# Down sums on another DMA queue, gated rows stored by quarters, and weights prepared a step earlier, in a decoder layer on one core

## The chip, the core and the metric

The kernel runs on one core of a Trainium2 chip. TensorE (PE) multiplies, VectorE (DVE), ScalarE (ACT) and GpSimd (POOL) work beside it, and SyncE (SP) issues most transfers between DRAM and the core's own memory; POOL issues the rest. The metric is the device time of one execution, in microseconds (us). The time before is 1876.97 us, the median of three runs (1875.70 to 1879.47).

## What is computed

One layer of a decoder, for a prompt of 1024 tokens and, with the same weights, for a group of 8 samples of one token each; together 1032 columns. Three branches (a gated linear recurrence, windowed attention, attention into a memory) are projected, gated and merged, and a gated feed-forward part follows. The change lies in that last part:

```python
D_MODEL, D_FF = 1024, 2816        # D_FF = 22 blocks of 128

def decoder_layer(x, ...):
    ...
    h = layer_norm(ALPHA * x + merged @ w_out, ln1_g, ln1_b)
    gt, up = jnp.split(h @ w_gate_up, 2, axis=-1)
    h = layer_norm(ALPHA * h + (jax.nn.silu(gt) * up) @ w_down, ln2_g, ln2_b)
    return h, conv_new, h_new, wk_new, wv_new
```

## The kernel before

**Layout and products.** Activations stand transposed, 128 features by 1032 columns. Each fp32 operand is split into a high and a low part: ACT casts the high part (L84), DVE subtracts it to get the low one (L85). A product is then three matmuls (high by high, high by low, low by high), each of 128 x 128 weights against 258 columns, a quarter of the 1032.

**Fast products.** A product of two by two blocks is made with seven block products in place of eight, of sums of weight blocks and sums of operand blocks; `fast_quarter` prepares the weights of one of the seven, i = 0 to 6, and `fast_step` multiplies and adds them up. In the gate and up projection two neighbouring units u = ("g", f) and v = ("g", f + 1), f even, share further products by the same scheme: `second_quarter`/`second_step` (steps "p0", "p1", "p4", "p6") and `fifth_quarter`/`fifth_step` ("v0", "v1", "v4", "v6"). Such a pair runs as

    (u,0) (prev v4) (u,1) (prev v6) (u,2) p0 (u,4) p1 (u,6) (v,0) p4 (v,1) p6 (v,2) v0 (v,4) v1 (v,6)

and takes about 39 us. "Pair 10" below is the pair with f = 10 and 11.

**The stage.** `gate_up_down` (L1600) works through pairs f = 2 to 21, then through the down products of blocks 0 to 15, in two parts of eight blocks. It fills about 1240 to 1790 us of the span. Its loop issues, at each step, the preparation of the weights `ahead` = 3 steps later (`quarter`), then the step's matmuls, then what falls due. Every engine works in the order in which it was issued; that order is fixed when the kernel is built. The prepared weights sit in rotating places: tag "qh" five, tag "ql" four, and one more "ql" in another pool (`half_pair`, L108).

**Gated rows.** When a unit's gate and up rows are complete, `FinishGate.done` (L2057) applies silu on ACT, multiplies on DVE (L2058) and stores the row, 128 x 1032, to DRAM (`scr["f"]`, L2059, on SP).

**Down sums.** The fast down product needs its operands, blocks of four rows by 258 columns, and sums of them. `down_block` (L1544) loads a block from four stored rows, in pieces of 258 columns (1032 bytes). `down_sums(part)` (L1551) is a generator: for p = 0 and 1 it loads b11, b12, b22, subtracts (L1563, L1565), stores, loads b21, adds (L1570), subtracts (L1573) and stores; the stores go to `scr["t"]` (L1558). Part 0 starts at f = 8 and part 1 at f = 16; a piece is issued after steps (u,2), (u,4) and (v,0). The first subtractions thus fall in pairs 8, 10, 16 and 18, after (v,0). All its loads and stores are on SP's queue. They use slots of `zt`, nine buffers of 128 x 1032 that gated rows use too, so a load into a slot waits until the store that last read it has landed. Later `down_operand` (L1579) loads blocks and sums for the product.

**What stands around it.** In `fast_step` at (v,0) DVE runs L389, which takes the result of earlier products out of PE's accumulator bank "pd" (tile pdfg). PE's product p4 (L1525 to L1527) begins a new sum in that bank and waits for L389. Blocks of a further scratch `t5` are loaded by `fifth_load` (L1417) for the products at L1465. `weight_means` (L1768) loads, in eight pieces of 128 x 768 into zt slots, the weights of the last six blocks and reduces them on DVE (L1777). Raw weights are loaded at L265.

Of the kernel before, what the change touches and what calls it, by code (L numbers as in the profile page):

```python
# [10 lines left out]
F32 = mybir.dt.float32  # L11
F32R = mybir.dt.float32r
# [7 lines left out]
P = 128  # L20
D = 1024
# [39 lines left out]
class Builder:  # L61
# [338 lines left out]
    def project(self, ctx, pool):  # L400

        nc, io, tc = self.nc, self.io, self.tc
        self.qdc = self.cst.tile([P, KT * NB], F32, name="qdc")
        self.qds = self.cst.tile([P, KT * NB], F32, name="qds")
        self.kd = self.cst.tile([P, 2 * NB], F32, name="kd")
        self.vd = self.cst.tile([NB, 256], F32, name="vd")
        self.lru_setup()
# [234 lines left out]
    def mem_scores(self, h, half, q, mk, between):  # L642

        nc = self.nc
        out = []
        for pr in range(2):
            s = self.bank("s", f"cs{h}_{half}_{pr}")
            for u in range(2):
                qt = pr * 2 + u
                self.mm3(s[:, u * 256:(u + 1) * 256], [  # L650
                    ((q[j][0][:, qt * P:(qt + 1) * P], q[j][1][:, qt * P:(qt + 1) * P]), mk[j]) for j in range(2)
                ])
            st = self.sm.tile([P, 8], F32, tag="cst", name=f"cst{h}_{half}_{pr}", bufs=4)
            p = self.ph.tile([P, 4 * 129], F32, tag="p", name=f"cp{h}_{half}_{pr}", bufs=4)[:, :512]
            nc.vector.tensor_reduce(st[:, 0:2], s.rearrange("p (a b) -> p a b", b=256), axis=AX.X,
                                    op=ALU.max, negate=True)
            for u in range(2):
                nc.scalar.activation(p[:, u * 256:(u + 1) * 256], s[:, u * 256:(u + 1) * 256], AF.Exp,
                                     bias=st[:, u:u + 1], scale=1.0, accum_out=st[:, 2 + u:3 + u])
            nc.vector.reciprocal(st[:, 4:6], st[:, 2:4])  # L660
            for u in range(2):
                nc.vector.tensor_scalar_mul(p[:, u * 256:(u + 1) * 256], p[:, u * 256:(u + 1) * 256],
                                            st[:, 4 + u:5 + u])
            out.append(p)
            if pr == 0:
                between()
        return out
# [108 lines left out]
    def win_scores(self, kv, ops, b, between=lambda: None):  # L776
# [6 lines left out]
        snk = self.nsnk[:, 4 * kv:4 * kv + 4]  # L783
        st = self.sm.tile([P, 12], F32, tag="bst", name=f"bst{kv}_{b}", bufs=4)
        p = self.ph.tile([P, 4 * 129], F32, tag="p", name=f"bp{kv}_{b}", bufs=4).rearrange("p (g n) -> p g n", g=4)
# [126 lines left out]
    def lru_consts(self):  # L912

        nc = self.nc
        lam = self.vec[:, V_LAM:V_LAM + KT]
        w = self.cst.tile([P, 8 * KT], F32, name="lruc")
# [3 lines left out]
        self.nsnk = self.cst.tile([P, 16], F32, name="nsnk")  # L920
        nc.vector.tensor_scalar_mul(self.nsnk, self.vec[:, V_SNK:V_SNK + 16], -1.0)
        self.hbg = self.cst.tile([P, 24], F32, name="hbg")
        nc.vector.tensor_scalar_mul(self.hbg, self.vec[:, V_BG:V_BG + 24], 0.5)
# [16 lines left out]
        nc.vector.tensor_scalar_mul(self.sp2, t, 2.0)  # L940
        self.sp4n = self.cst.tile([P, KT], F32, name="sp4n")
        nc.vector.tensor_scalar_mul(self.sp4n, t, -4.0)

    def lru_setup(self):
        self.scv = self.cst.tile([P, KT, 3, NB], F32, name="scv")
        self.scvo = self.cst.tile([P, KT, 3, NB], F32, name="scvo")
        self.sh = self.cst.tile([P, KT, NB], F32, name="sh")
        self.sho = self.cst.tile([P, KT, NB], F32, name="sho")
        self.pconv = self.cst.tile([P, KT, 3], F32, name="pconv")
        self.pho = self.cst.tile([P, KT], F32, name="pho")  # L950

# [83 lines left out]
    def dec_rows(self, qd, m0, dr, name):  # L1035

        nc = self.nc
        rows = self.sm.tile([NB, 256], F32, tag="drow", name=f"drow_{name}{m0}", bufs=1)
        ps = self.bank("o", f"drt_{name}{m0}")
# [5 lines left out]
    def dec_mem(self, h):  # L1045
# [45 lines left out]
        pr = ph.tile([NB, 256], F32, tag="dp", name=f"dcp{h}", bufs=1)  # L1091
        st = self.sm.tile([P, 8], F32, tag="cst", name=f"dcst{h}", bufs=4)
        nc.vector.tensor_reduce(st[:NB, 0:1], ps[:NB, :256], axis=AX.X, op=ALU.max, negate=True)
# [31 lines left out]
    def dec_win(self):  # L1125
# [7 lines left out]
        for name, row in (("o_swk", krow), ("o_swv", self.vd)):  # L1133
            nc.sync.dma_start(io[name][:, P - 1, :], row)
        work = self.sm.tile([P, 256], F32, tag="drow", name="dwork", bufs=1)
        qb, sc = work[:, :P], work[:, P:]
# [29 lines left out]
        pr = qb  # L1166
        st = self.sm.tile([P, 8], F32, tag="cst", name="dsst", bufs=4)
        snk = self.vec[:, V_SNKD:V_SNKD + 1]
# [8 lines left out]
        nc.vector.tensor_scalar_mul(sc, self.ident, pr[:, 0:1])  # L1177
        own = self.sm.tile([P, 8], F32, tag="cst", name="down", bufs=4)
        nc.vector.tensor_reduce(own, self.ident.rearrange("p (b r) -> p b r", b=NB), axis=AX.X, op=ALU.add)
# [148 lines left out]
    def plain_gate_up(self, f, h, steps):  # L1328
# [5 lines left out]
        for q in range(4):  # L1334
# [15 lines left out]
        nc.sync.dma_start(self.scr["f"][:, f, :], out)  # L1350
        self.zfree(out)
# [191 lines left out]

    def down_block(self, part, kh, th, p):  # L1544

        t = self.zt(f"f{part}{kh}{th}{p}")
        f0, t0 = 8 * part + 4 * kh, HT * th + QN * p
        self.nc.sync.dma_start(t.rearrange("p (k n) -> p k n", k=4), self.scr["f"][:, f0:f0 + 4, t0:t0 + QN])
        return t

    def down_sums(self, part):  # L1551


        tt = self.nc.vector.tensor_tensor
        for p in range(2):

            def keep(i, t):
                self.nc.sync.dma_start(self.scr["t"][:, part, p, (1, 2, 4, 6).index(i), :], t)  # L1558

            b11, b12 = (self.down_block(part, 0, th, p) for th in range(2))  # L1560
            b22 = self.down_block(part, 1, 1, p)
            yield
# [4 lines left out]
            self.zfree(b12)  # L1567
            b21 = self.down_block(part, 1, 0, p)
            yield
# [30 lines left out]
    def gate_up_down(self, ts):  # L1600
# [28 lines left out]
        todo = deque()  # L1629
        ahead = 3  # L1630

# [103 lines left out]
    def last_rows(self, home, j0):  # L1735

        flat = lambda t: t.rearrange("p k n -> p (k n)")
        for p, pair in enumerate(self.slot_pairs(home, f"g{home}")):
            hi, lo = map(flat, pair)
            self.nc.sync.dma_start(lo.bitcast(F32), self.scr["f"][:, LAST[0] + j0 + p, :])  # L1740
            self.g.append((hi, lo))
# [221 lines left out]
    def build(self):  # L1963
# [21 lines left out]
        with ExitStack() as right:  # L1985
            slots = right.enter_context(ExitStack())
            self.slots = [slots.enter_context(pool("slots0", "right"))]
            with pool("acc") as acc, pool("gp") as self.gp:
# [23 lines left out]
                with pool("slots1") as slots1:  # L2012
# [32 lines left out]
class FinishGate:  # L2045
# [9 lines left out]
    def done(self, za, zb):  # L2055
        b, nc = self.b, self.b.nc
        nc.scalar.activation(za, za, AF.Silu)  # L2057
        nc.vector.tensor_mul(za, za, zb)  # L2058
        nc.sync.dma_start(b.scr["f"][:, self.f, :], za)  # L2059
        b.zfree(za, zb)  # L2060
# [164 lines left out]
```

## Time and profile before

| | |
|---|---|
| median of three runs | 1876.97 us |
| the profiled execution, its own time | 1878.54 us |
| its span in the trace | 1876.8 us |
| granted TensorE clock, mean | 0.998 |
| DVE in the stage, 1240 to 1780 us | 416.2 of 540 us busy |
| blocks for down sums and products, loaded on SP (L1548) | 28 of 516 KB |
| POOL in the stage | 21 instructions, 18.0 us |

A busy time is the sum of an engine's instructions in the profiled execution. In a timeline a row has the start in us, the length in us, engine, line, operation, tile written and tiles read, their sizes, and in brackets the idle time of the engine just before and what ended it. "DMA to landing" is the time from the issue of a transfer until its last byte has landed, as minimum, median and maximum of a group. Tile names are the program's without numbers: z is a zt slot, pdfg the bank "pd", p1sfg a partial sum on DVE, ufg_2h and ufg_2l the high and low part of prepared weights, raw a raw weight block, s a sum of raw blocks, wsum a piece of the last blocks' weights.

### The profile page before, as it was taken

To read this page: it belongs to the slowest core of one execution; us is meant where nothing else is said; L and a number is where in the kernel's file an instruction comes from. 1 tells how busy PE (TensorE), PEld (TensorE's weight loads), DVE (VectorE), ACT (ScalarE), POOL (GpSimd) and SP (SyncE) were. 2 spreads that over 40 slices of the span, in tenths; PEclk is the share of its full clock that TensorE was granted. 3 is DMA by queue.
4 is the path that set the end of the run, shared out by engine and by line. 5 is a ranking of instruction groups with operands and counts; after the bars stand their busy time and mean duration, and the time that the engine had idled before them with its cause. 6 is when DMAs were issued, how large, how long until landed. Compare 5 with 4: busy or idle time off the path is not lost. (4 is left out here: it accounts for less than half of the span.)

```text
span 1876.8 us, 38124 instructions
## 1 busy us (share of the span) xinstructions
PE 1857.2 (99%) x14616; PEld 1839.9 (98%) x14616; DVE 1441.6 (77%) x2932; ACT 1055.0 (56%) x2250; POOL 123.3 (7%) x187
## 2 busy tenths in 40 slices
PE   9999999999999999999999999999999999999998
PEld 9999999999999999999999999999999999999998
DVE  7878878888789757568787567798787787857486
ACT  6576676665666756568774234544444434735355
POOL 1000002110000000021210000000000000001100
PEclk9999999999999999999999999999999999999999
DMA  9535345447344358647536251245586467866962
GB/s 337 171 115 175 110 143 168 137 139 263 119 160 168 121 195 272 212 128 238 173 99 190 91 192 57 69 167 183 183 272 205 154 216 246 262 169 188 206 184 91
DMA packets 186678, 326.93 MB, mean 174 GB/s; under 512 B 19760, under 2 KB 97536, under 8 KB 186496
## 3 DMA queue, kind: packets, MB, share of 16 engines
q1 hardware_dynamic: 179392, 304.86, 49.2%
q0 software_dynamic: 4224, 14.78, 3.9%
q10 hardware_dynamic: 2880, 4.85, 0.7%
q8 instruction: 115, 1.88, 0.4%
q14 instruction: 67, 0.55, 0.1%
HBM read 238.76 MB, written 89.84 MB: 175 GB/s over the span
## 5 line engine op out<-in xcount | busy, mean ns | idle before, releaser
L332 PE MATMUL ub<-th,u_6h 128*128 128x258 f32 x240 | 68.5, 285 | 1.3 <-DVE zb L380 0.6
L332 PE MATMUL ub<-th,u_2h 128*128 128x258 f32 x240 | 68.2, 284 | 0.9 <-ACT p1s L373 0.9
L332 PE MATMUL uc<-th,u_3h 128*128 128x258 f32 x240 | 68.1, 284 | 0.5 <-ACT v L503 0.5
L332 PE MATMUL ub<-th,u_4h 128*128 128x258 f32 x240 | 68.2, 284 | 0.2 <-ACT u2s L373 0.2
L332 PE MATMUL ud<-th,u_1h 128*128 128x258 f32 x240 | 68.1, 284 | 0.0
L334 PE MATMUL ud<-th,u_5l 128*128 128x258 f32 x240 | 68.1, 284 | 0.0
L332 PE MATMUL ud<-th,u_5h 128*128 128x258 f32 x240 | 68.1, 284 | 0.0
L332 PE MATMUL ub<-th,u_0h 128*128 128x258 f32 x240 | 68.1, 284 | 0.0
L334 PE MATMUL ub<-th,u_6l 128*128 128x258 f32 x240 | 68.1, 284 | 0.0
L334 PE MATMUL ub<-th,u_0l 128*128 128x258 f32 x240 | 68.1, 284 | 0.0
L334 PE MATMUL ud<-th,u_1l 128*128 128x258 f32 x240 | 68.1, 284 | 0.0
L334 PE MATMUL ub<-th,u_4l 128*128 128x258 f32 x240 | 68.1, 284 | 0.0
L334 PE MATMUL ub<-th,u_2l 128*128 128x258 f32 x240 | 68.1, 284 | 0.0
L334 PE MATMUL uc<-th,u_3l 128*128 128x258 f32 x240 | 68.0, 283 | 0.0
L333 PE MATMUL ub<-tl,u_6h 128*128 128x258 f32 x240 | 67.7, 282 | 0.0
L333 PE MATMUL ub<-tl,u_0h 128*128 128x258 f32 x240 | 67.7, 282 | 0.0
L333 PE MATMUL ud<-tl,u_5h 128*128 128x258 f32 x240 | 67.6, 282 | 0.0
L333 PE MATMUL ub<-tl,u_4h 128*128 128x258 f32 x240 | 67.6, 282 | 0.0
L333 PE MATMUL ud<-tl,u_1h 128*128 128x258 f32 x240 | 67.6, 282 | 0.0
L333 PE MATMUL ub<-tl,u_2h 128*128 128x258 f32 x240 | 67.6, 282 | 0.0
L333 PE MATMUL uc<-tl,u_3h 128*128 128x258 f32 x240 | 67.6, 282 | 0.0
L134 PE MATMUL op<-mh,woh 128*128 128x258 f32 x224 | 63.4, 283 | 0.0
(1080 smaller groups left out, 8228.8 us busy)
## 6 DMA issues: line engine op xcount, KB each, us to landing
ur<-win SPq DMA_DIRECT2D x120, 256.0 KB, 3.1
raw<-wgu SPq DMA_DIRECT2D x80, 256.0 KB, 3.5
t<-scr_t SPq DMA_DIRECT2D x36, 516.0 KB, 4.8
z<-scr_f SPq DMA_DIRECT2D x28, 516.0 KB, 4.8
scr_f<-z SPq DMA_DIRECT2D x22, 516.0 KB, 2.8
scr_t<-z SPq DMA_DIRECT2D x20, 516.0 KB, 3.2
raw<-wdn SPq DMA_DIRECT2D x35, 256.0 KB, 4.7
z<-scr_t SPq DMA_DIRECT2D x16, 516.0 KB, 8.8
```

The costliest lines, as they stand in the source:

```text
L134: nc.tensor.matmul(ps, sh, mh, start=opens and i == 0, stop=False)
L332: mm(sh[:, w], xh, start=opens and k == 0, stop=False)
L333: mm(sh[:, w], xl, start=False, stop=False)
L334: self.last_mm = mm(sl[:, w], xh, start=False, stop=k == 3).ins
```

## The change

1. Gated rows 0 to 15 go to a new scratch `scr["fq"]`, laid out by quarters of the columns, so that a block of four rows by 258 columns is one run of 4128 bytes. Storing a row now writes four runs of 1032 bytes (`keep_gated`). Rows 16 to 21 stay in `scr["f"]` as they were.
2. The 16 loads and 16 stores of `down_sums` are issued by POOL in place of SP. The loads in `down_operand` stay on SP.
3. `ahead` goes from 3 to 4; the places for prepared weights go to six each: a sixth "qh", and two "ql" beside the four, in pool w1.
4. Room for this: small constants and work tiles that are last used before the stage go to a pool `early`, closed ahead of the stage; `weight_means` loads 16 pieces of 128 x 384 into a buffer of its own and reduces each.

```diff
     def half_pair(self, name):
-        low = partial(self.wpool.tile, tag="ql", bufs=4)
+        high, low = (partial(self.wpool.tile, tag=f"q{e}", bufs=n) for e, n in (("h", 5), ("l", 4)))
         if self.sfree is not None:
             self.lows += 1
-            if self.lows % 5 == 0:
-                low = partial(self.w1.tile, tag="ql", bufs=1)
-        return self.wpool.tile([P, D // 2], F32R, tag="qh", name=f"{name}h", bufs=5), low([P, D // 2], F32R, name=f"{name}l")
+            if self.lows % 6 > 3:
+                low = partial(self.w1.tile, tag="ql", bufs=2)
+            if self.lows % 6 == 5:
+                high = partial(self.w1.tile, tag="qh", bufs=1)
+        return high([P, D // 2], F32R, name=f"{name}h"), low([P, D // 2], F32R, name=f"{name}l")
...
-        self.qdc = self.cst.tile([P, KT * NB], F32, name="qdc")
+        self.qdc = self.early.tile([P, KT * NB], F32, name="qdc")
...
-    def down_block(self, part, kh, th, p):
+    def keep_gated(self, f, z):
+
+        if f < 8 * FAST:
+            dst = self.scr["fq"][:, f // 4, :, f % 4 * QN:(f % 4 + 1) * QN]
+            return self.nc.sync.dma_start(dst, z.rearrange("p (q n) -> p q n", q=4))
+        return self.nc.sync.dma_start(self.scr["f"][:, f - 8 * FAST, :], z)
+
+    def down_block(self, part, kh, th, p, queue=None):
 
         t = self.zt(f"f{part}{kh}{th}{p}")
-        f0, t0 = 8 * part + 4 * kh, HT * th + QN * p
-        self.nc.sync.dma_start(t.rearrange("p (k n) -> p k n", k=4), self.scr["f"][:, f0:f0 + 4, t0:t0 + QN])
+        (queue or self.nc.sync).dma_start(t, self.scr["fq"][:, 2 * part + kh, 2 * th + p, :])
         return t
 
     def down_sums(self, part):
 
 
-        tt = self.nc.vector.tensor_tensor
+        tt, other = self.nc.vector.tensor_tensor, self.nc.gpsimd
         for p in range(2):
 
             def keep(i, t):
-                self.nc.sync.dma_start(self.scr["t"][:, part, p, (1, 2, 4, 6).index(i), :], t)
-
-            b11, b12 = (self.down_block(part, 0, th, p) for th in range(2))
-            b22 = self.down_block(part, 1, 1, p)
+                other.dma_start(self.scr["t"][:, part, p, (1, 2, 4, 6).index(i), :], t)
+
+            b11, b12 = (self.down_block(part, 0, th, p, other) for th in range(2))
+            b22 = self.down_block(part, 1, 1, p, other)
             yield
...
-            b21 = self.down_block(part, 1, 0, p)
+            b21 = self.down_block(part, 1, 0, p, other)
...
-        ahead = 3
+        ahead = 4
...
-        for m in range(KT):
-            z = self.zt(f"wsum{m}")
-            raw = z[:, :nf * P]
-            nc.sync.dma_start(raw, self.io["wdn"][m][:, f0 * P:(f0 + nf) * P])
+        n = nf // 2
+        for m, e in ((m, e) for m in range(KT) for e in range(2)):
+            raw = self.w1.tile([P, n * P], F32, tag="wsum", name=f"wsum{m}_{e}", bufs=1)
+            nc.sync.dma_start(raw, self.io["wdn"][m][:, (f0 + e * n) * P:(f0 + (e + 1) * n) * P])
             yield
-            nc.vector.tensor_reduce(part[:, m, :], raw.rearrange("p (k n) -> p k n", k=nf), axis=AX.X, op=ALU.add)
-            self.zfree(z)
+            nc.vector.tensor_reduce(part[:, m, e * n:(e + 1) * n], raw.rearrange("p (k n) -> p k n", k=n), axis=AX.X,
+                                    op=ALU.add)
             yield
...
+            first.close()
             with pool("zf") as self.z:
...
-        nc.sync.dma_start(b.scr["f"][:, self.f, :], za)
+        b.keep_gated(self.f, za)
         b.zfree(za, zb)
```

The lines of the kernel move by a few: L389 becomes L391, L1563, L1565, L1570 and L1573 become L1571, L1573, L1578 and L1581, L1525 becomes L1527.

How the order changes is seen at two places. The first is DVE in pair 10, around (v,0), from the first subtraction of the down sums to L389. Before (the numbers behind names are buffers):

```order
L1563 TENSOR_TENSOR z_14875<-z_14875,z_14874 128x1032
L85 TENSOR_TENSOR ufg_2l<-s_14868,ufg_2h 128x512
L1565 TENSOR_TENSOR z_14874<-z_14873,z_14874 128x1032
L306 TENSOR_TENSOR s_14868<-s_14868,raw_16551 128x512
L85 TENSOR_TENSOR ufg_v0l<-s_14866,ufg_v0h 128x512
L389 SCALAR_TENSOR_TENSOR p1sfg_1_18855<-pdfg_18724,p1sfg_1_18855 128x258
```

After:

```order
L1571 TENSOR_TENSOR z_14880<-z_14880,z_14876 128x1032
L1430 TENSOR_TENSOR s_14872<-s_14873 128x256
L1573 TENSOR_TENSOR z_14876<-z_14877,z_14876 128x1032
L85 TENSOR_TENSOR ufg_v0l<-s_14871,ufg_v0h 128x512
L1431 TENSOR_TENSOR s_14872<-s_14872,s_14871 128x256
L1578 TENSOR_TENSOR z_14877<-z_14877,z_14880 128x1032
L85 TENSOR_TENSOR ufg_4l<-s_14870,ufg_4h 128x512
L391 SCALAR_TENSOR_TENSOR p1sfg_1_18872<-pdfg_18741,p1sfg_1_18872 128x258
```

The low part of weights ufg_2 now comes ahead of the subtraction, and the preparation of the step after it (ufg_4) and the addition of the down sums stand between the subtraction and L391. The second place is the issue of the blocks for pair 10. Before, on SP, around the stores of rows 8 and 9 (the two rows scr_f<-z):

```order
L2059 DMA scr_f<-z_14871 128x1032
L1548 DMA z_14873<-scr_f 128x4x258
L265 DMA raw_16552<-wgu 128x512
L2059 DMA scr_f<-z_14874 128x1032
L1548 DMA z_14875<-scr_f 128x4x258
L1417 DMA t_18884<-scr_t_81 128x1032
L1548 DMA z_14874<-scr_f 128x4x258
```

After, on POOL, from the last transfers of the group before to the stores of the first two sums:

```order
L1566 DMA scr_t<-z_14874 128x1032
L1556 DMA z_14877<-scr_fq 128x1032
L1556 DMA z_14880<-scr_fq 128x1032
L1556 DMA z_14876<-scr_fq 128x1032
L1566 DMA scr_t<-z_14880 128x1032
L1566 DMA scr_t<-z_14876 128x1032
```

The blocks no longer stand between SP's other transfers; on POOL only transfers of the down sums stand in the row. The last load writes z_14876, the slot that row 9 is stored from, as the last load before wrote z_14874, the slot of row 9 there.

More of the change, by code (lines that the diff above doesn't have):

```diff
@@ L402, in project @@
         nc, io, tc = self.nc, self.io, self.tc
-        self.qdc = self.cst.tile([P, KT * NB], F32, name="qdc")
-        self.qds = self.cst.tile([P, KT * NB], F32, name="qds")
-        self.kd = self.cst.tile([P, 2 * NB], F32, name="kd")
-        self.vd = self.cst.tile([NB, 256], F32, name="vd")
+        self.qdc = self.early.tile([P, KT * NB], F32, name="qdc")
+        self.qds = self.early.tile([P, KT * NB], F32, name="qds")
+        self.kd = self.early.tile([P, 2 * NB], F32, name="kd")
+        self.vd = self.early.tile([NB, 256], F32, name="vd")
         self.lru_setup()
@@ L652, in mem_scores @@
                 ])
-            st = self.sm.tile([P, 8], F32, tag="cst", name=f"cst{h}_{half}_{pr}", bufs=4)
+            st = self.early.tile([P, 8], F32, tag="cst", name=f"cst{h}_{half}_{pr}", bufs=4)
             p = self.ph.tile([P, 4 * 129], F32, tag="p", name=f"cp{h}_{half}_{pr}", bufs=4)[:, :512]
@@ L783, in win_scores @@
         snk = self.nsnk[:, 4 * kv:4 * kv + 4]
-        st = self.sm.tile([P, 12], F32, tag="bst", name=f"bst{kv}_{b}", bufs=4)
+        st = self.early.tile([P, 12], F32, tag="bst", name=f"bst{kv}_{b}", bufs=4)
         p = self.ph.tile([P, 4 * 129], F32, tag="p", name=f"bp{kv}_{b}", bufs=4).rearrange("p (g n) -> p g n", g=4)
@@ L915, in lru_consts @@
         lam = self.vec[:, V_LAM:V_LAM + KT]
-        w = self.cst.tile([P, 8 * KT], F32, name="lruc")
+        w = self.early.tile([P, 8 * KT], F32, name="lruc")
         self.sp2 = w[:, 0:8]
@@ L919, in lru_consts @@
         e, z, z2, acc, t = (w[:, 24 + 8 * i:32 + 8 * i] for i in range(5))
-        self.nsnk = self.cst.tile([P, 16], F32, name="nsnk")
+        self.nsnk = self.early.tile([P, 16], F32, name="nsnk")
         nc.vector.tensor_scalar_mul(self.nsnk, self.vec[:, V_SNK:V_SNK + 16], -1.0)
-        self.hbg = self.cst.tile([P, 24], F32, name="hbg")
+        self.hbg = self.early.tile([P, 24], F32, name="hbg")
         nc.vector.tensor_scalar_mul(self.hbg, self.vec[:, V_BG:V_BG + 24], 0.5)
@@ L940, in lru_consts @@
         nc.vector.tensor_scalar_mul(self.sp2, t, 2.0)
-        self.sp4n = self.cst.tile([P, KT], F32, name="sp4n")
+        self.sp4n = self.early.tile([P, KT], F32, name="sp4n")
         nc.vector.tensor_scalar_mul(self.sp4n, t, -4.0)
     def lru_setup(self):
[L945 to L950, printed above, removed]
+        self.scv = self.early.tile([P, KT, 3, NB], F32, name="scv")
+        self.scvo = self.early.tile([P, KT, 3, NB], F32, name="scvo")
+        self.sh = self.early.tile([P, KT, NB], F32, name="sh")
+        self.sho = self.early.tile([P, KT, NB], F32, name="sho")
+        self.pconv = self.early.tile([P, KT, 3], F32, name="pconv")
+        self.pho = self.early.tile([P, KT], F32, name="pho")
     def load_lru(self):
@@ L1037, in dec_rows @@
         nc = self.nc
-        rows = self.sm.tile([NB, 256], F32, tag="drow", name=f"drow_{name}{m0}", bufs=1)
+        rows = self.early.tile([NB, 256], F32, tag="drow", name=f"drow_{name}{m0}", bufs=1)
         ps = self.bank("o", f"drt_{name}{m0}")
@@ L1091, in dec_mem @@
         pr = ph.tile([NB, 256], F32, tag="dp", name=f"dcp{h}", bufs=1)
-        st = self.sm.tile([P, 8], F32, tag="cst", name=f"dcst{h}", bufs=4)
+        st = self.early.tile([P, 8], F32, tag="cst", name=f"dcst{h}", bufs=4)
         nc.vector.tensor_reduce(st[:NB, 0:1], ps[:NB, :256], axis=AX.X, op=ALU.max, negate=True)
@@ L1134, in dec_win @@
             nc.sync.dma_start(io[name][:, P - 1, :], row)
-        work = self.sm.tile([P, 256], F32, tag="drow", name="dwork", bufs=1)
+        work = self.early.tile([P, 256], F32, tag="drow", name="dwork", bufs=1)
         qb, sc = work[:, :P], work[:, P:]
@@ L1166, in dec_win @@
         pr = qb
-        st = self.sm.tile([P, 8], F32, tag="cst", name="dsst", bufs=4)
+        st = self.early.tile([P, 8], F32, tag="cst", name="dsst", bufs=4)
         snk = self.vec[:, V_SNKD:V_SNKD + 1]
@@ L1177, in dec_win @@
         nc.vector.tensor_scalar_mul(sc, self.ident, pr[:, 0:1])
-        own = self.sm.tile([P, 8], F32, tag="cst", name="down", bufs=4)
+        own = self.early.tile([P, 8], F32, tag="cst", name="down", bufs=4)
         nc.vector.tensor_reduce(own, self.ident.rearrange("p (b r) -> p b r", b=NB), axis=AX.X, op=ALU.add)
@@ L1349, in plain_gate_up @@
                     next(steps, None)
-        nc.sync.dma_start(self.scr["f"][:, f, :], out)
+        self.keep_gated(f, out)
         self.zfree(out)
@@ L1739, in last_rows @@
             hi, lo = map(flat, pair)
-            self.nc.sync.dma_start(lo.bitcast(F32), self.scr["f"][:, LAST[0] + j0 + p, :])
+            self.nc.sync.dma_start(lo.bitcast(F32), self.scr["f"][:, LAST[0] - 8 * FAST + j0 + p, :])
             self.g.append((hi, lo))
@@ L1968, in build @@
                   "mk": [P, KT, NM], "mv": [P, KT, 256], "q": [KT, P, 2, TP], "k": [P, 2, 2, TP], "v": [P, 8, 512], "vd": [P, 8, 512],
-                  "h": [P, KT, T], "f": [P, NF, T], "t": [P, FAST, 2, 4, T],
+                  "h": [P, KT, T], "f": [P, NF - 8 * FAST, T], "fq": [P, 2 * FAST, 4, T], "t": [P, FAST, 2, 4, T],
                   "t5": [P, 4, T]}
         self.scr = {b: self.dram.tile(n, F32, name=f"scr_{b}") for b, n in shapes.items()}
-        self.cdec = self.cst.tile([P, KT, NB], F32, name="cdec")
         pool = lambda name, side="left": tc.tile_pool(name=name, bufs=1, side=side, reuse_waits="tile")
@@ L1975, in build @@
         self.ctx.enter_context(pool("edge", "right")).tile([P, 8], F32, name="edge")
+        first = ExitStack()
+        self.early = first.enter_context(pool("early"))
+        self.cdec = self.early.tile([P, KT, NB], F32, name="cdec")
         self.zbufs, self.sum_bufs, self.zslots, self.sfree = 9, 3, None, None
```

## Prediction

> **What bounds the kernel now.** I read the page first, for the engine that never rests and for the engine whose work the last chain is made of.
>
> ```profile
> span 1876.8 us, 38124 instructions
> PE 1857.2 (99%) x14616; PEld 1839.9 (98%) x14616; DVE 1441.6 (77%) x2932; ACT 1055.0 (56%) x2250; POOL 123.3 (7%) x187
> PE 15%; DMA 0%; DVE 0%; issue 0%; DVEq 0%; ACT 0%
> ```
>
> PE is busy for 99% of the span, and the chain that ended last is PE's own (the shares are small because the chain is followed back only to a wait in the stage that the change touches). No matmul is added or removed, so the time can move only by PE's waits. Second, the table by windows, for the stage of the change, and third, PE's waits over the whole span.
>
> ```profile
> 1240.00:1780.00 540.00, 535.59 (x4438) 534.28 (x4437) 416.21 (x746) 244.71 (x464) 17.99 (x21) 1.00 0.68 207
> PE pdfg L1525 <- DVE p1sfg L389: 3.6, 3, 1.8
> PE qbfg L1465 <- DMA t<-scr_t: 0.8, 1, 0.8
> ```
>
> In 540 us PE has 4.4 us without a matmul, and these two rows are all of it: three waits for L389 on DVE, one for a block that SP loads. The granted clock is 1.00. The rest of PE's waits lie ahead of the stage or behind it, in code that stays. PE starts a matmul each 540/4438 = 0.122 us, while each is shown as 0.28 long, so the true loss at a wait is what is printed plus 0.16. Fourth, PE's timeline at the four waits and at one smaller one.
>
> ```profile
> 1375.09 0.28 PE L334 MATMUL udfg<-hth,ufg_1l 128*128 128x258 f32 x1
> 1375.36 0.39 PE L1525 MATMUL pdfg<-hh,ufg_p4h 128*128 128x258 f32 x1
> ...
> 1416.06 0.39 PE L1525 MATMUL pdfg<-hh,ufg_p4h 128*128 128x258 f32 x1 [1.77 <-DVE p1sfg L389]
> ...
> 1534.67 0.38 PE L1525 MATMUL pdfg<-hh,ufg_p4h 128*128 128x258 f32 x1 [0.89 <-DVE p1sfg L389]
> ...
> 1574.63 0.39 PE L1525 MATMUL pdfg<-hh,ufg_p4h 128*128 128x258 f32 x1 [0.92 <-DVE p1sfg L389]
> ...
> 1593.42 0.36 PE L1465 MATMUL qbfg<-t,ufg_v4h 128*128 128x258 f32 x1 [0.83 <-DMA t<-scr_t]
> ```
>
> The losses are 1.93, 1.05 and 1.08 us at the pairs that begin with f = 10, 16 and 18, and 1375.36 - 1375.09 - 0.12 = 0.15 at pair 8: 4.21 us at L1525. The fifth is 0.99 us at L1465. So the change can win about 5.2 us, 0.28%, and no more.
>
> Why L389 is late is read from DVE's timeline at those places.
>
> ```profile
> 1411.48 1.23 DVE L1563 TENSOR_TENSOR z<-z,z 128x1032 f32<-128x1032 f32 x1 [3.92 <-DMA z<-scr_f]
> ...
> 1415.58 0.42 DVE L389 SCALAR_TENSOR_TENSOR p1sfg<-pdfg,p1sfg 128x258 f32<-128x258 f32 x1
> ...
> 1528.28 1.23 DVE L1563 TENSOR_TENSOR z<-z,z 128x1032 f32<-128x1032 f32 x1 [1.50 <-DMA z<-scr_f]
> ...
> 1534.19 0.42 DVE L389 SCALAR_TENSOR_TENSOR p1sfg<-pdfg,p1sfg 128x258 f32<-128x258 f32 x1
> ...
> 1570.05 1.23 DVE L1563 TENSOR_TENSOR z<-z,z 128x1032 f32<-128x1032 f32 x1 [3.08 <-DMA z<-scr_f]
> 1571.20 0.68 DVE L85 TENSOR_TENSOR ufg_2l<-s,ufg_2h 128x512 fp32r<-128x512 f32 x1
> 1571.80 1.23 DVE L1565 TENSOR_TENSOR z<-z,z 128x1032 f32<-128x1032 f32 x1
> ...
> 1574.15 0.42 DVE L389 SCALAR_TENSOR_TENSOR p1sfg<-pdfg,p1sfg 128x258 f32<-128x258 f32 x1
> 1574.48 0.42 DVE L1428 TENSOR_TENSOR s<-s 128x256 f32<-128x256 f32 x1
> 1574.82 0.42 DVE L1536 SCALAR_TENSOR_TENSOR z<-pbfg,p1sfg 128x258 f32<-128x258 f32 x1
> ```
>
> DVE works in order. Its first subtraction of the down sums, L1563, waits 3.92, 1.50 and 3.08 us for a block from DRAM, and L389, which needs nothing of that block, stands behind it. PE starts 1574.63 - 1574.15 = 0.48 after L389. The same rows give what each kind of step holds DVE: 1.15 us for 1032 columns (1570.05 to 1571.20), 0.60 for 512, 0.34 for 256. Why the block is late is on SP's timeline.
>
> ```profile
> 1362.08 0.32 SPq L2059 DMA_DIRECT2D scr_f<-z  x1
> ...
> 1401.39 0.32 SPq L2059 DMA_DIRECT2D scr_f<-z  x1
> ...
> 1405.08 0.37 SPq L1548 DMA_DIRECT2D z<-scr_f  x1
> ...
> 1520.63 0.32 SPq L2059 DMA_DIRECT2D scr_f<-z  x1
> ...
> 1524.28 0.93 SPq L1548 DMA_DIRECT2D z<-scr_f  x2
> ...
> 1560.77 0.32 SPq L2059 DMA_DIRECT2D scr_f<-z  x1
> ...
> 1564.46 0.37 SPq L1548 DMA_DIRECT2D z<-scr_f  x1
> ```
>
> The last load of a group is issued 3.69, 3.65 and 3.69 us after the store of a gated row: it takes that row's buffer (or, in group 16, reads the row itself), so it waits until the store has landed. From its issue to L1563 pass 6.40, 4.00 and 5.59 us, 5.33 in the mean.
>
> **The change part by part.** *The store that the last load waits for stays.* In the new order the load issued on POOL waits for the same stores: at pair 10 it takes the buffer of row f = 9, at 16 it reads rows 14 and 15, at 18 it takes the buffer of row 17. These rows come from a silu and a product that no edit moves. I keep 3.67 us from store to load. The store now writes four runs of 1032 bytes instead of one of 4128 for a row; the load reads in one run what was four. I take both at nothing; they act against each other, and their sizes don't change.
>
> *The load goes to POOL.* What I need is L, the time from its issue until L1563 (L1571 now) can start. POOL issues no load of this kind in the stage before; its nearest rows are one plain load of the same size and the adding ones.
>
> ```profile
> L1548 SPq DMA_DIRECT2D z<-scr_f x28: 370/378/951, 1338.1 to 1701.0; - x28
> DMA to landing us min/median/max: 3.6/4.8/6.2
> ...
> L1764 POOL DMA_DIRECT2D z<-scr_h x1: 572/572/572, 1722.2 to 1722.2; - x1
> DMA to landing us min/median/max: 5.1/5.1/5.1
> ...
> L1766 POOL DMA_DIRECT2D z<-scr_h x7: 866/878/886, 1739.9 to 1789.9; - x7
> DMA to landing us min/median/max: 5.5/6.5/10.0
> ```
>
> The plain load took 5.1 us on POOL against SP's median of 4.8, 0.3 more. I add this to the mean of the three places: L = 5.6 (bounds 3.6, SP's fastest, and 6.5, the median of the loads that also add). A lone row is thin ground, so both ends stay in the range.
>
> [...]
>
> *Four steps ahead puts more between the load and L389.* With weights prepared a step earlier, DVE's row has at pairs 10, 16 and 18 seven steps from the first subtraction to L389 (L391 now): 1032, 256, 1032, 512, 256, 1032 and 512 columns, 3 x 1.15 + 2 x 0.34 + 2 x 0.60 = 5.33 us. Before it was 1415.58 - 1411.48 = 4.10, then 5.91, then 4.10. So two places get 1.23 worse and one 0.58 better, in sum 1.9 worse. At pair 8 two subtractions stand there, 2.30.
>
> PE's arrival at L1525 is its start less idle less 0.16: 1414.13, 1533.62 and 1573.55. The new order moves the first p4 product on that bank by one matmul, 0.12 later at pairs 10 and 18, 0.12 earlier at 16 and 8. The loss at pair 10 is then 1401.39 + 3.67 + L + 5.33 + 0.48 - 1414.25 = L - 3.38; at 16, with 1520.63 and 1533.50, L - 3.39; at 18, with 1560.77 and 1573.67, L - 3.42. At pair 8 it is 1362.08 + 3.67 + L + 2.30 + 0.48 - 1375.09 = L - 6.56, none here. The sum is 3 x (5.6 - 3.40) = 6.6 us against 4.21 before: **+2.4 us**. Each 1 us of L is worth 3; the change breaks even at L = 4.8. The bounds 3.6 and 6.5 give -3.6 and +5.1.
>
> *The block for L1465.* Before, SP issued it as soon as PE was done with the tile's last use:
>
> ```profile
> 1581.00 4.86 SPq L265 DMA_DIRECT2D raw<-wgu  x3
> 1586.12 1.45 SPq L1417 DMA_DIRECT2D t<-scr_t  x2
> ```
>
> It took 7.17 us instead of the median 4.8 because weights went out just ahead. In the new order SP comes to it behind a load of a sum (L1596) that waits for DVE's split of an earlier block, and that block's buffer is free only when POOL's store has landed. Worked from the rows: first subtraction at 1570.0 plus some, POOL's store behind the second, about 5 us to land, 4.8 for the next block, 2 us of split: 1587 to 1588 against 1586.12, while PE comes to it 1.2 us later too. I take 0; bounds -1.0 (no wait left) and +2.
>
> *Edits at nothing.* Sixteen reduces of half the size for eight, and their own buffer: DVE is busy 416 of 540 us, and they stand between steps where it waits; uncovered, they would cost what one more instruction adds, some 0.1 each. The pool of small constants adds no instruction. SP loses 32 DMAs, about 0.4 to 0.9 us of issue each, beside waits of its own. The fourth step prepared ahead shows as casts that PE and DVE no longer wait for, on rows like this:
>
> ```profile
> DVE ufg_2l L85 <- ACT ufg_2h L84: 21.8, 11, 2.7
> ```
>
> That is slack of DVE alone: PE has no wait for a cast in this stage. At the stage's start one more quarter is made before the first step, a cast and a subtraction, 1.3 us at most if PE waited; nothing there waits now, so 0.
>
> The sum is +2.4 us on the profiled execution's own 1878.54, 1880.9. That execution is 1.57 above the median of the runs, 1876.97, so on the median it is **1879.4 us**, 0.13% more.
>
> **The rivals.** *Early blocks (24%).* POOL's queue has nothing else to do, while SP's loads went out among weight loads, and its 4.00 at pair 16 shows what a free moment gives. If L is about 3.4 to 3.6, the three waits are gone and the result is -3.6 to -4.2: 1872.8 to 1873.4, and 1871.8 if the wait at L1465 goes as well. Against it stands POOL's only plain row, 5.1. [...]
>
> *Late blocks on POOL (22%).* The slower side. Place: the subtractions ahead of L391 at pairs 10, 16 and 18. Price: three times what L has above 4.8. It decides from L = 6.05, where the sum is 3 x 2.65 - 4.21 = +3.75; at 6.5, as the adding loads have in the median, it is +5.1: 1882.1. For it: the DMA engines are 0.68 busy in the stage and SP's own load took 6.40 at pair 10. Against it: the adding loads do more than a plain one.
>
> *The block for L1465 behind SP's new waits (13%).* With the forecast's +2.4 and 2 us there: 1881.4.
>
> *Nothing moves* is inside the forecast: the last load still waits for the same store, and with L = 4.8 the time is that of before.
>
> **How the numbers follow.** The forecast, L between about 4 and 6, has 41%. A measurement of this kernel can tell about 0.2% from no change, 3.75 us. Of the early case 18 of the 24 parts pass that bound; the other 6 stay within it, with the 41 of the forecast. The late case and that of L1465 pass it on the other side, 35 together. So faster 18%, same 47%, slower 35%. The range runs from 1873.0, nearly all of the waits gone, to 1884.0, which is +5.1 and 2 us at L1465; about one part in ten is left out on each side.
>
> **What would show it.** In the new profile, the first subtraction, L1571, should still wait for a DMA at pairs 10, 16 and 18, and PE at L1527 behind L391 for about 2.2 us at each, alike, since the distance is now the same at all three; pair 10 hardly changes (1.93), 16 and 18 double. POOL's block loads should land in 5 to 6 us. If the subtraction waits for nothing, the early case holds. The prediction is wrong if the stores of the gated rows come earlier, if L is under 4, or if PE waits at a place that it doesn't wait at now, above all at the stage's start or at L1465.

## The result and the profile after

The changed kernel takes 1890.99 us (median of four runs, 1887.71 to 1892.37) against 1877.35 of before beside it: ratio 1.0064, 95% interval 1.0052 to 1.0076 (the quotient of the two medians, 1.0073, lies within it). The forecast was 1879.4 with a range to 1884.0, and a time that does not change as the likeliest case. It got slower, for the larger part by the mechanism of the forecast at the places it named, and by more than its dearest case.

The head of the page after, the span and the engines' busy times:

```profile
span 1889.8 us, 38158 instructions
PE 1860.5 (98%) x14616; PEld 1843.4 (98%) x14616; DVE 1440.4 (76%) x2940; ACT 1055.8 (56%) x2250; POOL 139.6 (7%) x219
```

PE's waits, with the total, the number and the longest:

```profile
PE pdfg L1527 <- DVE p1sfg L391: 12.3, 4, 5.7
PE ubfg L334 <- DVE z L369: 1.5, 1, 1.5
```

The span grew by 13.0 us, and the wait for L391 from 3.6 to 12.3. The wait for the block at L1467 (L1465 before) is gone, and one for L369 is new. PE's timeline at the places of it:

```profile
1403.47 0.39 PE L334 MATMUL ubfg<-hth,ufg_4h 128*128 128x258 f32 x1 [1.48 <-DVE z L369]
...
1421.46 0.58 PE L1527 MATMUL pdfg<-hh,ufg_p4h 128*128 128x258 f32 x1 [5.66 <-DVE p1sfg L391]
1421.84 0.42 PE L1528 MATMUL pdfg<-hl,ufg_p4h 128*128 128x258 f32 x1
1422.06 0.42 PE L1529 MATMUL pdfg<-hh,ufg_p4l 128*128 128x258 f32 x1
...
1544.83 0.39 PE L1527 MATMUL pdfg<-hh,ufg_p4h 128*128 128x258 f32 x1 [3.46 <-DVE p1sfg L391]
...
1588.60 0.39 PE L1527 MATMUL pdfg<-hh,ufg_p4h 128*128 128x258 f32 x1 [3.02 <-DVE p1sfg L391]
```

With 0.16 added to each as in the prediction, the losses at pairs 10, 16 and 18 are 5.82, 3.62 and 3.18 us, where 2.2 each was forecast. Behind the first, PE's matmuls follow each other at 0.21 us in place of 0.12. The table by windows shows why (columns: window, its length, busy time and count of PE, PEld, DVE, ACT and POOL, granted clock, share of the DMA engines, GB/s):

```profile
1421.00:1427.00 6.00, 5.54 (x26) 5.54 (x27) 3.97 (x10) 1.90 (x4) 0.41 (x1) 0.52 0.26 103
1427.00:1430.00 3.00, 3.00 (x27) 3.00 (x26) 2.80 (x5) 0.62 (x1) 0.00 (x0) 1.00 0.19 66
1546.00:1550.00 4.00, 4.00 (x23) 4.00 (x22) 2.66 (x6) 1.98 (x5) 0.00 (x0) 0.57 0.64 193
```

After the long wait PE's clock was granted at 0.52, and 26 matmuls took the time of some 45; from 1546, a microsecond after the second wait, the same happened for 16. That is about 2.4 and 1.5 us more. DVE's timeline, at the reduce that waits ahead of 1403, and then from the first subtraction to L391 at pairs 10, 16 and 18:

```profile
1395.11 0.55 DVE L1785 TENSOR_REDUCE wpart<-wsum 128x3 f32<-128x384 f32 x1 [4.53 <-DMA wsum<-wdn]
...
1415.67 1.24 DVE L1571 TENSOR_TENSOR z<-z,z 128x1032 f32<-128x1032 f32 x1 [1.28 <-DMA z<-scr_fq]
...
1420.99 0.42 DVE L391 SCALAR_TENSOR_TENSOR p1sfg<-pdfg,p1sfg 128x258 f32<-128x258 f32 x1
...
1539.04 1.23 DVE L1571 TENSOR_TENSOR z<-z,z 128x1032 f32<-128x1032 f32 x1 [3.34 <-DMA z<-scr_fq]
...
1544.36 0.42 DVE L391 SCALAR_TENSOR_TENSOR p1sfg<-pdfg,p1sfg 128x258 f32<-128x258 f32 x1
...
1582.81 1.23 DVE L1571 TENSOR_TENSOR z<-z,z 128x1032 f32<-128x1032 f32 x1 [2.89 <-DMA z<-scr_fq]
...
1588.12 0.42 DVE L391 SCALAR_TENSOR_TENSOR p1sfg<-pdfg,p1sfg 128x258 f32<-128x258 f32 x1
```

The distance is 5.32, 5.32 and 5.31 us, as worked out. What the forecast missed lies ahead of the subtraction: the stores on SP and the last loads on POOL.

```profile
1399.33 0.38 SPq L1550 DMA_DIRECT2D scr_fq<-z  x1
1399.81 1.45 SPq L1419 DMA_DIRECT2D t<-scr_t  x1
1401.33 0.42 SPq L267 DMA_DIRECT2D raw<-wgu  x1
1403.10 0.37 SPq L1550 DMA_DIRECT2D scr_fq<-z  x1
...
1528.32 0.37 SPq L1550 DMA_DIRECT2D scr_fq<-z  x1
...
1572.53 0.32 SPq L1551 DMA_DIRECT2D scr_f<-z  x1
```

```profile
1403.48 0.54 POOL L1556 DMA_DIRECT2D z<-scr_fq  x1 [3.24 <-DVE z L369]
1411.85 0.53 POOL L1556 DMA_DIRECT2D z<-scr_fq  x1 [7.83 <-DMA scr_fq<-z]
...
1534.67 1.16 POOL L1556 DMA_DIRECT2D z<-scr_fq  x2 [39.40 <-DMA raw<-wgu]
...
1577.98 0.53 POOL L1556 DMA_DIRECT2D z<-scr_fq  x1 [4.52 <-DMA scr_f<-z]
```

From the store to the load that the first subtraction uses pass 8.75, 6.35 and 5.45 us where 3.7 passed before. (At pair 16 that is the first of two loads in one row; the second follows 6.98 us after the store, the figure that the first expectation below quotes.) At pairs 10 and 18 POOL's own row names the store as what it waited for; at pair 16 it names a load of weights, and that the store held the load there is inferred, since the block holds the row just stored. From that load to the subtraction it is then 3.82, 4.37 and 4.83 us, less than the 5.6 of the forecast. So the sum from store to subtraction is 12.57, 10.72 and 10.28 us, against 10.09, 7.65 and 9.28 before and a forecast of 9.27.

### The profile page after: what moved, and what is told of

Its sections match the earlier page's. It is cut to its first block, busy times and chain, and to the rows that moved or that the text cites. A ratio compares the mean times of both kernels' runs of the same rounds, so it can differ in the third digit from the quotient of the medians.

```text
span 1889.8 us, 38158 instructions
## 1 busy us (share of the span) xinstructions
PE 1860.5 (98%) x14616; PEld 1843.4 (98%) x14616; DVE 1440.4 (76%) x2940; ACT 1055.8 (56%) x2250; POOL 139.6 (7%) x219
## 5 line engine op out<-in xcount | busy, mean ns | idle before, releaser
L334 PE MATMUL ub<-th,u_6h 128*128 128x258 f32 x240 | 68.5, 285 | 1.8 <-DVE zb L382 1.1
L334 PE MATMUL ub<-th,u_4h 128*128 128x258 f32 x240 | 68.2, 284 | 0.3 <-ACT u2s L375 0.3
L334 PE MATMUL ub<-th,u_0h 128*128 128x258 f32 x240 | 68.1, 284 | 0.0
L334 PE MATMUL ud<-th,u_5h 128*128 128x258 f32 x240 | 68.1, 284 | 0.0
L334 PE MATMUL uc<-th,u_3h 128*128 128x258 f32 x240 | 68.0, 283 | 0.0
L334 PE MATMUL ud<-th,u_1h 128*128 128x258 f32 x240 | 68.0, 283 | 0.0
L334 PE MATMUL ub<-th,u_2h 128*128 128x258 f32 x240 | 68.0, 283 | 0.0
```

The lines of the kernel that those rows point to most:

```text
L334: mm(sh[:, w], xh, start=opens and k == 0, stop=False)
```

## The experiments

Ratios are to the kernel before, run on the same chip beside each (its medians there lie between 1877.35 and 1879.29 us). Losses are PE's in the profiled execution, at the first p4 product on bank "pd" (L1525, or L1527) with 0.16 added; 0 where none is to be seen.

| run | time, us | ratio, 95% interval | loss at pairs 8, 10, 16, 18, us | store to subtraction at 10, 16, 18, us |
|---|---|---|---|---|
| before | 1877.35 | 1 | 0.15, 1.93, 1.05, 1.08 | 10.09, 7.65, 9.28 |
| changed | 1890.99 | 1.0064 (1.0052 to 1.0076) | 0.34, 5.82, 3.62, 3.18 | 12.57, 10.72, 10.28 |
| sums back on SP | 1884.83 | 1.0029 (1.0016 to 1.0042) | 0.43, 2.41, 2.73, 1.15 | 10.09, 9.83, 9.21 |
| three steps ahead | 1891.24 | 1.0067 (1.0044 to 1.0091) | 0.27, 6.41, 2.82, 3.41 | |
| layout and POOL alone | 1899.34 | 1.0106 (1.0082 to 1.0129) | 5.20, 5.60, 3.34, 4.58 | 12.44, 10.20, 11.45 |
| layout alone | 1879.82 | 1.0008 (0.9999 to 1.0017) | 0, 1.68, 1.81, 2.09 | 9.84, 8.41, 10.28 |
| changed, whole means | 1893.16 | 1.0084 (1.0058 to 1.011) | 5.42, 5.67, 2.78, 2.44 | |
| changed, sums behind L391 | 1881.35 | 1.0012 (1.0001 to 1.0024) | 0, 4.38, 0, 0 | |
| the same, whole means | 1875.36 | 0.9975 (0.9964 to 0.9986) | 0, 0.49, 0.61, 0 | |
| before, sums behind L389 | 1875.78 | 0.9981 (0.997 to 0.9992) | 0, 0, 0, 0 | |
| layout and POOL, sums behind L389 | 1877.69 | 0.9997 (0.9988 to 1.0006) | 0, 0, 0, 0 | |
| layout and POOL, rows on POOL too | 1909.55 | 1.016 (1.0143 to 1.0177) | 8.09, 6.35, 6.46, 5.55 | |

### Which part of the change

**The sums back on SP's queue**, the rest as changed:

```diff
-        tt, other = self.nc.vector.tensor_tensor, self.nc.gpsimd
+        tt, other = self.nc.vector.tensor_tensor, self.nc.sync
```

> The changed kernel with one thing undone: the 16 loads and 16 stores of the down sums go back to SP's queue. Theory (POOL's queue is the cause: its load waits longer for the store of the gated row, 8.75, 6.98 and 5.45 us at pairs 10, 16, 18 in place of 3.7, and the order on DVE gets worse): store to load falls to 3.7 to 4.5, the losses at L1527 to about 1.6, 0.6 and 1.6 us, the slow matmuls behind the long waits go, the 1.65 us wait of pair 10 for DVE's reduce stays: 1877 to 1881 us. Rival A (preparing four steps ahead, or the traffic of the new weight means, is the cause): the three losses stay near 5.8, 3.6 and 3.2 us, 1888 to 1892 us.

The time fell by 0.35% but not to that of before: 1884.83, between the two expectations. PE's wait for L391 in that run:

```profile
PE pdfg L1527 <- DVE p1sfg L391: 7.2, 5, 2.6
```

It is 7.2 us, between 3.6 before and 12.3 after; the fifth wait is a new one at pair 14, a loss of 1.27 us. DVE's timeline at pair 10:

```profile
1412.11 1.23 DVE L1571 TENSOR_TENSOR z<-z,z 128x1032 f32<-128x1032 f32 x1 [2.15 <-DMA z<-scr_fq]
```

The subtraction of pair 10 stands 10.09 us behind its store again, as before. From store to load pass 5.42, 4.43 and 3.23 us at the three places, with the same layout as the changed kernel's 8.75, 6.35 and 5.45. The wait at L334 in pair 10, which the theory kept, is not there. About half of the loss of time goes with POOL's queue; the rest stays with the other parts.

**Three steps ahead**, the rest as changed:

```diff
-        ahead = 4
+        ahead = 3
```

> The changed kernel with ahead = 3 again, places and all else as changed. Theory: the rows of DVE between the first subtraction and L391 are the same seven (5.33 us) with three steps ahead, so the losses stay near 5.8, 3.6, 3.2 us: 1888 to 1893 us. Rival (the prediction's reason, that the fourth step puts more in between): 1.2 us less at pairs 10 and 18, 1885 to 1888 us; rival A in full: 1877 to 1881 us.

PE's wait in that run:

```profile
PE pdfg L1527 <- DVE p1sfg L391: 12.2, 3, 6.3
```

1891.24 us, as the theory said, with 5.31 us from the subtraction to L391 at all three places and a wait for L391 as long as in the changed kernel (12.3). The number of steps is not what puts L391 far behind the subtraction.

**Layout and POOL alone**, on the kernel before: `keep_gated`, `down_block` and `down_sums` of the change, with three steps ahead, five and four places, whole means.

> The kernel before with the quarter layout and the down sums on POOL, and nothing else of the change. DVE's order then has 5.8 us between the first subtraction and L389 at pairs 8, 10, 16 and 18. Theory: store to load and load to use together 10.3 to 12.6 us as in the changed kernel, losses of 3 to 5.5 us at three pairs and slow matmuls behind them: 1887 to 1895 us. Rival A: together 9.0 us as before, losses of 2.4 us at three pairs, no slow matmuls: 1879 to 1882 us.

It is the slowest of the parts, 1899.34 us, slower than the whole change and than the theory, which had losses at three pairs and not at four. Who waits for the blocks, by the view of their line, L1554 (L1569 is the first subtraction there):

```profile
who waited for it (us, times):
  DVE z L1569: 21.4, 4
```

POOL's timeline has the last load of pair 10:

```profile
1417.55 0.53 POOL L1554 DMA_DIRECT2D z<-scr_fq  x1 [7.76 <-DMA scr_fq<-z]
```

The subtraction waits at all four pairs, 21.4 us against 8.5 us at three before, and the load has waited 7.76 us for the store. DVE's order takes 5.9 us to L389 at all four, and PE's matmuls are 0.21 us apart for a while behind each of the four waits. So the queue, with the order that the kernel's build gives it, makes the loss; the layout without it, next, does not.

**Layout alone**, all on SP:

> The kernel before with the quarter layout alone; all transfers on SP as before, and DVE's rows at the four pairs as before. Theory: within 1.5 us of before, losses near 1.9, 1.0 and 1.1 us, store to load 3.7 us. Rival (stores in four runs land later and are part of the long way from store to load): store to load above 4.5 us at pairs 10 and 16, 1880 to 1884 us.

The time stays: 1.0008, with an interval that holds 1. SP's timeline at pair 10, store and last load:

```profile
1400.06 0.37 SPq L1548 DMA_DIRECT2D scr_fq<-z  x1
...
1405.56 0.32 SPq L1554 DMA_DIRECT2D z<-scr_fq  x1
```

DVE's timeline, the subtraction that uses it:

```profile
1409.90 1.24 DVE L1569 TENSOR_TENSOR z<-z,z 128x1032 f32<-128x1032 f32 x1 [3.67 <-DMA z<-scr_fq]
```

Both expectations are half right. Store to load is longer at pairs 10 and 16, 5.50 and 4.79 us against 3.69 and 3.65, as the rival said; at pair 18, where the row is still stored in one run, it is 3.66. At pair 10 the load is shorter by as much, 4.34 against 6.40. At pairs 16 and 18 the sum is 0.8 and 1.0 us longer than before, and the four losses add up to 5.58 us against 4.21. The layout gives nothing, and what it costs, some 1.4 us, is not clear of the noise.

**The whole means**: eight loads of 128 x 768 into zt slots, as before the change; the rest as changed.

```diff
-        n = nf // 2
-        for m, e in ((m, e) for m in range(KT) for e in range(2)):
-            raw = self.w1.tile([P, n * P], F32, tag="wsum", name=f"wsum{m}_{e}", bufs=1)
+        for m in range(KT):
+            z = self.zt(f"wsum{m}")
+            raw = z[:, :nf * P]
...
```

> The changed kernel with the eight whole loads of the weight means in zt slots again. Theory: the waits of DVE's reduces for their pieces (4.53 and 4.72 us) go and with them the 1.65 us at pair 10; the three losses at L1527 stay: 1887 to 1890 us. Rival (the pieces' traffic is what makes row 9's store take 8 us): store to load at pair 10 falls under 6 us, its loss to about 2.7 us and the slow matmuls behind it go: 1882 to 1885 us.

1893.16 us, above both expectations. The wait at L334 in pair 10 went. Store to load at pair 10 is still 8.28 us, so the pieces' traffic is not what delays it, and the rival falls. But pair 8, which lost 0.34 in the changed kernel, now loses 5.42: the order on DVE changed there too, and the subtraction came to wait, on DVE's timeline:

```profile
1372.28 1.23 DVE L1571 TENSOR_TENSOR z<-z,z 128x1032 f32<-128x1032 f32 x1 [5.13 <-DMA z<-scr_fq]
```

Undoing one part moves the loss, as long as L391 stands behind that subtraction.

### Is it the place of L391

**The changed kernel, with the subtractions kept behind L391.** The order is forced by an edge without a wait; nothing else is touched in the source, but the build then orders some other instructions anew.

```diff
-            nc.vector.scalar_tensor_tensor(st["s", 0, 1], st["pd"]["p", 1], scale, st["s", 0, 1], op0=ALU.mult,
-                                           op1=ALU.subtract)
+            self.pd_taken = nc.vector.scalar_tensor_tensor(st["s", 0, 1], st["pd"]["p", 1], scale, st["s", 0, 1],
+                                                           op0=ALU.mult, op1=ALU.subtract).ins
...
-            if (i in (2, 4) and where[u] % 2 == 0 or i == 0 and where[u] % 2) and sums and next(sums[0], self) is self:
-                sums.popleft()
+            if (i in (2, 4) and where[u] % 2 == 0 or i == 0 and where[u] % 2) and sums:
+                with self.tc.issue_after(self.pd_taken) if i == 0 else nullcontext():
+                    if next(sums[0], self) is self:
+                        sums.popleft()
```

> The changed kernel, with the subtractions of the down sums kept behind L391 on DVE by an order alone (an edge without a wait); queue, layout, places and four steps ahead as changed. Theory (PE loses its time at L1527 because L391 stands behind a subtraction whose block is late): the losses of 5.8, 3.6 and 3.2 us and the slow matmuls behind them go, blocks land as late as before: 1874 to 1879 us, with up to 1.7 us left at pair 10 for DVE's reduce. Rival (the late block then holds the next steps of DVE, which free the banks of p6 and v0): the waits of PE move a few matmuls down, 1881 to 1888 us.

1881.35 us: the losses at 16 and 18 are gone, that at 10 is still 4.38, so the time missed the theory's range and lies at the low end of the rival's. DVE's timeline at pair 10:

```profile
1413.88 0.56 DVE L1787 TENSOR_REDUCE wpart<-wsum 128x3 f32<-128x384 f32 x1 [4.09 <-DMA wsum<-wdn]
...
1417.43 0.55 DVE L1787 TENSOR_REDUCE wpart<-wsum 128x3 f32<-128x384 f32 x1 [0.42 <-DMA wsum<-wdn]
...
1420.40 0.55 DVE L1787 TENSOR_REDUCE wpart<-wsum 128x3 f32<-128x384 f32 x1 [0.69 <-DMA wsum<-wdn]
1421.74 0.42 DVE L391 SCALAR_TENSOR_TENSOR p1sfg<-pdfg,p1sfg 128x258 f32<-128x258 f32 x1
1422.08 1.22 DVE L1571 TENSOR_TENSOR z<-z,z 128x1032 f32<-128x1032 f32 x1
```

The subtraction now follows L391 and waits for nothing, so what is left is not the rival's late block. In its place three reduces of the weight means stand ahead of L391, each for a piece that can be loaded only when the single buffer is free of the one before. That is a second wait of the same kind, which the first had hidden.

**The same, with the whole means:**

> The changed kernel with the subtractions kept behind L391 and, in addition, the weight means in eight whole loads in zt slots. Theory (what is left in the run that did the first alone, 4.4 us at pair 10 with slow matmuls behind it and 1.6 us ahead of it, comes from DVE's reduces, which wait for pieces that go through one buffer one after the other, ahead of L391): all of it goes, about 8 us of the profile: 1873 to 1878 us. Rival (blocks on POOL's queue hold PE in another way, or the reduces are as late in whole pieces): 1879 to 1883 us as in that run.

1875.36 us, as the theory said: with POOL's queue, layout, places and four steps ahead as changed, the kernel is faster than before. The stage by windows:

```profile
1240.00:1790.00 550.00, 548.13 (x4546) 546.88 (x4545) 421.69 (x761) 252.41 (x479) 36.22 (x54) 1.00 0.68 210
```

PE is busy for all but 1.9 us of 550.

**The kernel before, with the same order alone:**

> The kernel before with the same order alone. Theory: the losses of 1.93, 1.05, 1.08 and 0.15 us at L1525 go, that of 0.99 us at L1465 stays: 3.5 to 4.5 us less than before. Rival (the late block holds the next steps of DVE): within 1 us of before.

The same window in that run:

```profile
1240.00:1790.00 550.00, 549.23 (x4553) 548.28 (x4552) 424.11 (x763) 251.51 (x478) 18.21 (x21) 1.00 0.68 209
```

PE lacks 0.8 us here. The ratio of 0.9981 is some 3.6 us, near the 4.21 of the losses at L1525. The wait at L1465 went too, and 0.74 us came at another place. The order alone does as much as the run above with the whole change in addition (0.9975; the intervals overlap), so no gain of queue, layout, places or fourth step is shown.

**Layout and POOL alone, with the same order:**

> The kernel before with quarter layout and POOL's queue for the down sums, as in the run before that did this alone (1899.34 us), and in addition the subtractions kept behind L389. Theory: the four waits of 3.3 to 5.6 us go, 1874 to 1881 us. Rival (POOL's transfers slow the others, at whatever place): 1885 to 1895 us.

1877.69 us in place of 1899.34, as the theory said. At pair 10 the subtraction stands behind L389 now, and still waits a little for its block, on DVE's timeline:

```profile
1414.14 0.42 DVE L389 SCALAR_TENSOR_TENSOR p1sfg<-pdfg,p1sfg 128x258 f32<-128x258 f32 x1
1414.82 1.23 DVE L1569 TENSOR_TENSOR z<-z,z 128x1032 f32<-128x1032 f32 x1 [0.26 <-DMA z<-scr_fq]
```

POOL's transfers do little harm in themselves (0.9997, with 0.9981 for the same order without them). 21.7 us hang on whether an instruction of 0.42 us stands ahead of the subtractions or behind them. The largest loss left in the stage is of the same kind on another engine, by ACT's and PE's timelines:

```profile
1607.39 1.06 ACT L84 CAST d00h<-z 128x1032 fp32r<-128x1032 f32 x1 [6.82 <-DMA z<-scr_fq]
...
1612.63 0.38 PE L332 MATMUL ubfg<-hh,ufg_0h 128*128 128x258 f32 x1 [2.52 <-ACT z L2061]
```

ACT's cast waits 6.82 us for a block that SP loads for the down products, and L2061, which takes a result out of one of PE's banks, stands behind it. PE loses 2.68 us there, and 16 slow matmuls follow a microsecond later, some 1.5 us more.

### Why the store lands late

**The stores of the rows on POOL's queue too** (all but the first two rows), on the kernel with layout and POOL alone:

```diff
-        b.keep_gated(self.f, za)
+        b.keep_gated(self.f, za, nc.gpsimd)
```

> The kernel before with quarter layout and the down sums on POOL (as in the run that did this alone: store of row 9 to the last load 8.67 us, 1899.34 us), and the stores of the gated rows on POOL's queue too, so that they no longer stand behind blocks and weights that SP sent out ahead. DVE still has 5.8 us from the first subtraction to L389 at pairs 10, 16 and 18. Theory S1 (the store lands late because it queues behind SP's transfers): store to load 4 to 6 us at these pairs, losses of 2 to 3 us each: 1882 to 1890 us. Theory S2 (it lands late because both queues' transfers share the same engines at that moment, whatever the queue): store to load 7.5 to 9 us at pair 10, 6 at the others: 1895 to 1901 us.

1909.55 us, worse than both expected. From store to load pass 8.29, 5.89, 5.21 and 7.10 us at pairs 8, 10, 16 and 18, against 5.76, 8.67, 5.33 and 6.04 with the rows on SP: in the mean no less. The larger loss comes from ahead of that. With the rows on SP a store is issued 0.03 us after DVE has made the row; here at pairs 8, 10 and 16 it is 3.3 to 3.9 us, since POOL's queue comes to it late. DVE's and POOL's timelines at pair 8:

```profile
1362.31 1.23 DVE L2064 TENSOR_TENSOR z<-z,z 128x1032 f32<-128x1032 f32 x1
...
1366.80 0.56 POOL L1554 DMA_DIRECT2D z<-scr_fq  x1 [5.83 <-DMA scr_fq<-z]
1367.45 0.75 POOL L1548 DMA_DIRECT2D scr_fq<-z  x1
```

The row is done at 1363.54, and its store stands behind a load that waits for the store before it. The view of the stores' line in that run:

```profile
L1548 POOL DMA_DIRECT2D scr_fq<-z x14: 754/768/808, 1281.7 to 1543.3; - x14
...
DMA to landing us min/median/max: 3.0/6.1/8.5
```

The traces show the landing of only three or four stores on SP in each run, too few to set beside this median. So the run does not separate the two theories: taking the stores off SP's queue did not bring the loads nearer to them, and put a new wait ahead of them. How the delay divides between SP's transfers ahead of the store (a block t and a weight block within the 3.3 us ahead, above) and POOL's loads beside it stays open.

## Why the prediction was wrong

**The bound and the places: right.** PE's waits in the stage decide, and those at pairs 10, 16 and 18 for L391, behind a subtraction that waits for a block, carry the change. That runs with the subtractions behind L391 lose this wait shows it.

**The distance from the subtraction to L391: right in size, wrong in its reason.** 5.33 us was worked out and 5.31 to 5.32 measured. But the prediction gave the fourth step ahead as the reason; with three steps the waits are the same. With the sums on POOL alone DVE's order takes 5.9 us there, and with layout alone 4.10, 5.9 and 4.10; in the changed kernel with the sums back on SP it measures 3.91, 5.31 and 4.71. The order goes with the queue, at two of the three places.

**The step that failed: "The store that the last load waits for stays. ... I keep 3.67 us from store to load."** The edge stayed, its length did not: 8.75, 6.35 and 5.45 us. Two things lengthen it. The store in four runs, which the prediction took at nothing, makes it 5.50, 4.79 and 3.66 with all transfers on SP (layout alone), where the load gave this back at pair 10. POOL's queue on the same layout makes it 8.67, 5.33 and 6.04. I had put all of POOL's uncertainty into L, from the load's issue on, and L turned out shorter than taken, 4.34 in the mean against 5.6. The sum of both was 11.19 us in the mean against 9.27, 1.92 more, three times: 5.8 us. With it the formula gives 3 x (11.19 + 5.33 + 0.48) less PE's arrivals, 12.54, 12.89 and 12.89 after the stores, 12.7 us for the measured 12.6, where 6.6 was forecast. Two of the prediction's own signs of being wrong showed: L was under 4 at pair 10, and PE waits at a place where it did not, L334. The late rival had the place and the price right and its point of decision in the wrong term.

**A term that was missing: the clock.** A wait was counted at its own length. Two of the three were followed by matmuls 0.21 us apart in place of 0.12 (granted clock 0.52 and 0.57 in the windows above), some 3.9 us in all.

**A term at nothing that was not: the weight means.** "They stand between steps where it waits" counted the reduces' own time (0.55 us for a piece, 0.94 for a whole load) and not that each waits, in DVE's order, for a piece through a single buffer. It cost 1.64 us in pair 10 of the changed kernel (with the sums back on SP that wait is gone, so it hangs on the queue too), and some 6 us once the subtractions were out of the way (medians of 1881.35 with the pieces, 1875.36 whole).

**The block for L1465:** taken at 0 with a bound of -1.0; it came to the bound.

The account of the 13.0 us: at L1527 12.96 (with 0.34 at pair 8) less 4.21 gives +8.8, the slow matmuls +3.9, L334 +1.6, L1465 -1.0: 13.3.

**The early case** did not come: from the issue of POOL's last load to the subtraction passed 3.8 us at the fastest of the three places, and the longer delay lies ahead of the issue. Nothing was won by the move to POOL's queue (layout alone 1.0008, with POOL in addition 1.0106).

## What to carry to other kernels

Where an engine works in order, look for an instruction that PE waits for and that stands behind one that waits for a transfer: here moving it ahead was worth more than the transfer's new queue and layout, and made these harmless. When a transfer is moved to another queue, price the whole way from what it waits for to who uses it, since the transfers that stay may land later (at pair 10 the load that waits for the store was issued 8.67 us behind it with layout and POOL alone, 5.50 with layout alone), and read the new order of the engine that consumes it. A wait that is removed can uncover a second one of its kind, so undo parts in pairs before a part is judged.

## What the runs showed of the hardware

After the longest waits PE ran at about half its clock for a few microseconds: in the changed kernel the granted clock was 0.52 from 1421 to 1427, where the wait of 5.66 us ends, and 1.00 in the 3 us behind that. Every wait of 4.38 us or more at the p4 product, with 0.16 added as in the table (twelve in these runs), was followed at once by 12 to 26 matmuls 0.21 us apart. Of the nine between 2.4 and 3.7 us four were followed by such matmuls (2.41, 2.82, 3.34 and 3.62), partly a microsecond late, as from 1546 above, where the granted clock was 0.57 over 4 us; five were not (2.44, 2.73, 2.78, 3.18 and 3.41), and shorter ones never were. What decides between 2.4 and 3.7 us stays open.
